# A feed-forward's operand preparation: token halves normed through PSUM, and the first two jobs in another order of products

## The chip, the cores and the metric

One core of one Trainium2 chip runs the whole program as one launch. The metric is the device time in microseconds (us). TensorE is called PE here, VectorE DVE, ScalarE ACT, GpSimd POOL; SP starts the DMAs. [...]

## The reference, cut to what matters

The model has two layers, each a token mixer followed by a feed-forward. There are 512 latent and 256 context tokens of 1024 channels. Only the feed-forward is touched by the change:

```python
def rmsnorm(x, g):
    y = x32 * lax.rsqrt(jnp.mean(x32 * x32, axis=-1, keepdims=True) + NORM_EPS)
    return (y * g.astype(jnp.float32)).astype(x.dtype)
def swiglu(h, w1, w3, w2):
    return (jax.nn.silu(h @ w1) * (h @ w3)) @ w2
...
    x = x + ga_f * swiglu(rmsnorm(x, g_ffn[i]) * (1.0 + sc_f) + sh_f, w1[i], w3[i], w2[i])
```

Layer 0 runs it for all 768 tokens, layer 1 for the 512 latent ones only.

## The kernel before

Activations are stored with the channels on the partitions, in eight tiles of 128 channels, and the tokens along the free axis. An fp32 operand of a matmul is split into a high part (`hi`, a cast by ACT) and a low part (`lo`, the rest, a subtraction on DVE or POOL), and each product is three matmuls in PSUM (L398, L399, L400: hi by hi, hi by lo of the weight, lo by hi). Weights are split likewise (L183 the cast, L188 the lo).

The up-projections `h @ w1` and `h @ w3` are done by a Strassen scheme (Winograd's form). A job is a pair of 128-column blocks of w1 or of w3; the channels are halved (tiles 0 to 3 and 4 to 7) and the tokens are halved, so that the activations are four blocks: B11 and B12 (first half of the channels), B21 and B22 (second half). Seven products p = 1 to 7 replace eight. Products 1 and 2 need B11 and B21, the first token half; p = 3 needs B22; p = 6, 7, 4 and 5 need sums of blocks, called T here: T1 = B12 - B11, T2 = B22 - T1 (p = 6), T3 = B22 - B12 (p = 7), T4 = T2 - B21 (p = 4); p = 5 takes T1. A product is 12 matmuls, 4 chunks of channels by 3, on 384 columns in layer 0 and 256 in layer 1.

PE must be kept busy while the second half's norm and those sums come about. So the four jobs that lead (w1 and w3, two each) do P1 and then P2 together (`first_products`, 48 matmuls each), chunk by chunk, and between the chunks the generator `prepare` is asked for its next steps, as often as the table `PREP` says. The PSUM results of P1 are copied out by ACT (`complete`, L1592), those of P2 wait in PSUM. The first two jobs then do p = 6, 7, 4, 5, 3, and what follows is ordered by a planner with due times (`in_order`), which the change does not touch.

`first_norm` makes the operands of P1 and P2 for the first half: DVE scales a tile (L1471), ACT adds the shift into SBUF (L1479), ACT casts it (L1492), and DVE and POOL take turns at the lo (L1496). `prepare` does the second half: RMS (`rstd`, with L615 its reciprocal), the scaling and shift of both channel halves of one index, T1 (L1515) and T2 (L1517) on DVE, the cast of T2 (L1523), and its lo and T4 on POOL (L1524, L1525). After four indices come T3 (L1528) for all four, and then the operands of p = 7, 4, 5, 3 in four steps (`put`, L1461 the cast, L1462 the lo).

The sums of weight blocks for p = 6 (L225 to L227, a tile S and two others) and p = 7 (L229) are made on DVE by `form`, ahead of their use where room is short; the lo of w1 for p = 7 of the first job is on DVE too. All instructions of an engine run in the order of the code; semaphores tie the engines together. PSUM has 8 banks, dealt out in turn, and a bank's new owner waits for the last reader of the old one. Results go through L1596, L1599, L1603 (sums of products), L1630 and L1634 (sum into a block), L1635 (times the gate).

Of the kernel before, what the change touches and what calls it, by code (L numbers as in the profile page):

```python
# [41 lines left out]
PREP = (0, 1, 1, 2), (1, 1, 1, 2)  # L42
# [4 lines left out]
STEPS = (1, 2, 6, 7, 4, 5, 3)  # L47
NCOL = 0.4219
# [10 lines left out]
class Job:  # L59
# [42 lines left out]
class WeightStream:  # L102
# [6 lines left out]
    def __init__(self, kern, raws, parts):  # L109
# [7 lines left out]

        self.lead, self.dve = {}, {}
# [6 lines left out]

    def add_step(self, job, p, aps):
# [4 lines left out]
        if 1 in self.USES[p] and job.units[1] is None:  # L131
# [19 lines left out]
    def there(self, task):  # L151
# [4 lines left out]
        return all(i in what.raw or what.units[i] in self.raw for i in self.USES[p])  # L156
# [54 lines left out]
    def form(self, job, p):  # L211
# [5 lines left out]
        for i in self.USES[p]:  # L217
            if i not in job.raw:
                job.raw[i] = self.raw.pop(job.units[i])
        n = job.n = job.raw[0].shape[-1] // 2  # L220
        (a11, a12), (a21, a22) = ((t[:, :n], t[:, n : 2 * n]) for t in (job.raw[0], job.raw.get(1, job.raw[0])))
        if p == 6:
# [5 lines left out]
        if p == 7:  # L228
            v.tensor_sub(a12, a12, a11)  # L229
# [1134 lines left out]
class FeedForward:  # L1364
# [10 lines left out]
    def plan(self):  # L1375
# [27 lines left out]
        for j in two:  # L1403
            j.steps = ()
        self.order = [(j, p) for p in (1, 2) for j in lead] + [(j, p) for p in STEPS[2:] for j in two]
# [29 lines left out]
    def begin(self, x, acc, streams, out):  # L1435
# [3 lines left out]
        self.h = [None] * NK  # L1439
# [24 lines left out]
    def scaled(self, rs, st, i):  # L1464

        k = self.k
        if self.h[i] is None:
            self.h[i] = k.act(name="hf")
        t = k.tmp(name="hn")
        for s, sl, at in pieces(st):  # L1470
            k.nc.vector.scalar_tensor_tensor(  # L1471
                t[:, at], self.x[i][:, sl], k.gs[:, self.layer, 1, s, i : i + 1], rs[:, at], op0=OP.mult, op1=OP.mult
            )
        return t

    def shifted(self, t, st, i):
        k = self.k
        for s, sl, at in pieces(st):
            k.nc.scalar.activation(self.h[i][:, sl], t[:, at], AF.Identity, bias=k.mod[:, self.layer, 3, s, i : i + 1])  # L1479

    def first_norm(self):
        st, n = self.streams[0], self.n
        nc = self.k.nc
        rs = yield from self.k.rstd(self.acc[st], st[1])
        yield 0
        for i in range(NK + 1):
            j = i - 1
            if i < NK:
                t = self.scaled(rs, st, i)
            if i > 0:  # L1490
                hi, lo = self.operand(1 + j // 4, j % 4)
                nc.scalar.copy(hi, self.h[j][:, :n])  # L1492
            if i < NK:
                self.shifted(t, st, i)
            if i > 0:
                (nc.gpsimd if j % 2 else nc.vector).tensor_sub(lo, self.h[j][:, :n], hi.bitcast(F32))  # L1496
                yield 0

    def prepare(self):

        st, n = self.streams[1], self.n
        nc = self.k.nc
        v = nc.vector
        rs = yield from self.k.rstd(self.acc[st], st[1], False)
        yield 0

        def block(e, i):
            return self.h[i + 4 * (e // 2)][:, n * (e % 2) : n * (e % 2) + n]

        for i in range(5):  # L1510
            if i < 4:
                ts = [(j, self.scaled(rs, st, j)) for j in (i, i + 4)]
            if i > 0:
                b11, b12, b21, b22 = (block(e, i - 1) for e in range(4))
                v.tensor_sub(b11, b12, b11)  # L1515
                t2 = self.k.tmp(name="T2")[:, :n]
                v.tensor_sub(t2, b22, b11)  # L1517
            if i < 4:
                for j, t in ts:
                    self.shifted(t, st, j)  # L1520
            if i > 0:
# [726 lines left out]
```

## Time and profile before

| | us |
|---|---|
| three runs | 1699.68, 1704.15, 1704.51 |
| median | 1704.15 |
| the profiled execution | 1700.14, of which the span of the trace is 1698.4 |
| PE busy in the span | 1601.1 (94%) |
| DVE, POOL, ACT busy | 1178.8 (69%), 818.6 (48%), 741.9 (44%) |

The span runs from the first instruction to the last; every time below counts from its start. The feed-forward's lead runs from about 448 to 520 us in layer 0 and from 1309 to 1368 us in layer 1. A timeline row is one instruction, or several like it in a row ("x4", with their time together); in brackets stands how long the engine had stood idle before it and which instruction ended that wait. A duration is longer than the distance to the next instruction where work is pipelined: the matmuls of 384 columns last 0.33 us and start every 0.17 us.

### The profile page before, as it was taken

How to read it: one execution, taken by the hardware profiler on the slowest of the kernel's cores; microseconds unless marked ns; L12 is line 12 of the kernel's file. 1: busy time of each engine (PE TensorE's matmuls, PEld its weight loads, DVE VectorE, ACT ScalarE, POOL GpSimd, SP SyncE). 2: the span in 40 equal slices, each digit the busy share in tenths (PEclk: the TensorE clock that was granted, in tenths of full speed). 3: DMA queues.
4: the chain of work that ended last, by engine and by line, in shares of the span. 5: the costliest groups of instructions: out<-in, count | busy, mean ns of one | idle time of the engine just before them, and what ended most of it. 6: DMA issues, size and time to landing. Idle time of an engine off the chain costs nothing. (4 is left out here: it accounts for less than half of the span.)

```text
span 1698.4 us, 26272 instructions
## 1 busy us (share of the span) xinstructions
PE 1601.1 (94%) x9730; PEld 1449.0 (85%) x9730; DVE 1178.8 (69%) x2054; ACT 741.9 (44%) x1437; POOL 818.6 (48%) x601
## 2 busy tenths in 40 slices
PE   6989999999979998999999999999999799999996
PEld 4867788888979987899999997779789789999996
DVE  6866566773777899586766776665666876766685
ACT  5534444653553223242332554444554544344343
POOL 3443232123375556465555623444125676666672
PEclk9999999999989999999999999999999899999998
DMA  9364253353023343434443345422232132332322
GB/s 355 139 199 138 67 160 97 119 170 130 26 76 111 103 134 120 129 125 137 149 137 118 127 161 163 135 73 74 80 131 81 60 115 75 111 114 76 94 87 69
DMA packets 76384, 202.28 MB, mean 119 GB/s; under 512 B 12704, under 2 KB 19488, under 8 KB 75872
## 3 DMA queue, kind: packets, MB, share of 16 engines
q1 hardware_dynamic: 76256, 200.60, 36.5%
q8 instruction: 77, 1.26, 0.3%
q14 instruction: 51, 0.42, 0.1%
HBM read 184.25 MB, written 11.80 MB: 115 GB/s over the span
## 5 line engine op out<-in xcount | busy, mean ns | idle before, releaser
L188 POOL TENSOR_TENSOR wp<-wr,wp 128x512 fp32r<-128x512 f32 (+1 forms) x336 | 465.7, 1399 | 311.0 <-ACT wp L183 306.2
L398 PE MATMUL f<-hp,wp 128*128 128x384 f32 (+1 forms) x1232 | 386.8, 314 | 14.8 <-DVE U L1599 4.2
L399 PE MATMUL f<-hp,wp 128*128 128x384 f32 (+1 forms) x1232 | 387.1, 314 | 10.8 <-DVE wp L188 6.2
L400 PE MATMUL f<-hp,wp 128*128 128x384 f32 (+1 forms) x1232 | 385.2, 313 | 4.0 <-POOL hp L1524 4.0
L183 ACT CAST wp<-wr 128x512 fp32r<-128x512 f32 (+1 forms) x360 | 213.3, 609 | 309.4 <-PE f L400 118.5
L188 POOL TENSOR_TENSOR wl<-wr,wh 128x1024 fp32r<-128x1024 f32 (+2 forms) x75 | 163.8, 2188 | 346.4 <-ACT wh L183 266.4
L398 PEld LDWEIGHTS f<-hp,wp 128*128 128x128 f32 x1232 | 238.0, 193 | 18.8 <-issue 8.2
L399 PEld LDWEIGHTS f<-hp,wp 128*128 128x128 f32 x1232 | 238.4, 193 | 15.3 <-POOL wp L188 8.5
L400 PEld LDWEIGHTS f<-hp,wp 128*128 128x128 f32 x1232 | 238.1, 193 | 5.1 <-POOL hp L1524 5.1
L398 PE MATMUL proj<-h,wh 128*128 128x512 f32 (+1 forms) x456 | 165.0, 362 | 1.0 <-DVE v L404 1.0
L398 PE MATMUL f<-g,wp 128*128 128x512 f32 (+1 forms) x468 | 160.5, 343 | 5.4 <-ACT g L1461 5.4
L400 PE MATMUL f<-g,wp 128*128 128x512 f32 (+1 forms) x468 | 160.5, 343 | 0.0
L399 PE MATMUL f<-g,wp 128*128 128x512 f32 (+1 forms) x468 | 160.3, 342 | 0.0
L399 PE MATMUL proj<-h,wl 128*128 128x512 f32 (+1 forms) x456 | 159.1, 349 | 0.7 <-POOL wl L188 0.7
L400 PE MATMUL proj<-h,wh 128*128 128x512 f32 (+1 forms) x456 | 158.9, 348 | 0.0
L1658 DVE SCALAR_TENSOR_TENSOR x<-f,mod,x 128x512 f32<-128x512 f32 (+1 forms) x130 | 79.0, 622 | 69.5 <-PE f L400 69.3
L398 PEld LDWEIGHTS proj<-h,wh 128*128 128x128 f32 x456 | 86.6, 190 | 25.5 <-issue 6.6
L522 DVE CUSTOM_DVE_ANT_0 adj<-wr,tab 128x1024 bf16<-128x1024 f32 x64 | 104.6, 1653 | 4.1 <-DMA wr<-in_w_adat_dram 4.0
L398 PEld LDWEIGHTS f<-g,wp 128*128 128x128 f32 x468 | 89.1, 190 | 17.0 <-ACT g L1461 6.8
L400 PEld LDWEIGHTS f<-g,wp 128*128 128x128 f32 x468 | 88.9, 190 | 11.2 <-DVE g L1462 1.1
L399 PEld LDWEIGHTS f<-g,wp 128*128 128x128 f32 x468 | 89.1, 190 | 9.9
L399 PEld LDWEIGHTS proj<-h,wl 128*128 128x128 f32 x456 | 86.8, 190 | 11.8 <-POOL wl L188 1.1
(251 smaller groups left out, 3415.2 us busy)
## 6 DMA issues: line engine op xcount, KB each, us to landing
wr<-in_w_dram SPq DMA_DIRECT2D x88, 512.0 KB
wr<-in_w_adat_dram SPq DMA_DIRECT2D x48, 512.0 KB
wr<-in_w_dram SPq DMA_DIRECT2D x80, 256.0 KB
wr<-in_w_ada_dram SPq DMA_DIRECT2D x32, 512.0 KB
ada<-in_w_ada_dram SPq DMA_DIRECT2D x16, 512.0 KB
wr<-in_w_out_dram SPq DMA_DIRECT2D x16, 512.0 KB
tab<-in_rpb_dram SPq DMA_DIRECT2D x12, 512.0 KB
strip<-strips SPq DMA_DIRECT2D x3, 1152.0 KB
```

The lines of the kernel that those rows point to most:

```text
L183: nc.scalar.copy(hi, src)
L188: (nc.vector if vector else nc.gpsimd).tensor_sub(lo, src, hi.bitcast(F32))
L398: mm(out, a[0], b[0], start=start, stop=False)
L399: mm(out, a[1], b[0], start=False, stop=False)
L400: mm(out, a[0], b[1], start=False, stop=stop)
L522: self.nc.vector.tensor_tensor_reduce(out=self.tmp(mybir.dt.bfloat16, D, "adj"), in0=raw, in1=self.tabs[("silu", s)], scale=1.0, scalar=0. ...
L1658: k.nc.vector.scalar_tensor_tensor(xs, ps[:, :n], k.mod[:, self.layer, 5, s, m : m + 1], xs, op0=OP.mult, op1=OP.add)
```

## The change

Four things are done to the preparation of the operands.

- `first_norm` writes the scaled tile into a PSUM bank. ACT reads it twice, once for the fp32 copy and once for the cast, and all the lo are on DVE, from PSUM.
- `prepare` first finishes B22 (a loop over channel tiles 4 to 7: scaled by DVE, scale and shift on ACT, cast on ACT, lo on POOL), which is p = 3's operand. Then come four blocks; in each, ACT writes B12 into a PSUM bank, DVE takes T3 = B22 - bank, turns the bank into T1, ACT copies T1 out, DVE turns the bank into T2, casts and lo follow, and T4 is taken on DVE. Last, the operands of p = 5 and p = 4.
- The first two jobs go p = 3, 7, 6, 4, 5 (`FIRST`). So that p = 3 can come first, all four sums of weight blocks are made ahead of it, and P1's result is copied out twice for these two jobs.
- `PREP` asks for one step fewer after the last chunk of P1.

```diff
-PREP = (0, 1, 1, 2), (1, 1, 1, 2)
+PREP = (0, 1, 1, 1), (1, 1, 1, 2)
+FIRST = (3, 7, 6, 4, 5)
...
-        if p == 6:
+        if p == job.first:
             job.s1 = self.k.tmp(name="S1")[:, :n]
...
-        if p == 7:
+        if p == (3 if job.first == 3 else 7):
             v.tensor_sub(a12, a12, a11)
...
+            if self.held and task[1] is self.held and task[0][1] == self.held.first:
+                self.issue()
+                break
...
-        self.order = [(j, p) for p in (1, 2) for j in lead] + [(j, p) for p in STEPS[2:] for j in two]
+        self.order = [(j, p) for p in (1, 2) for j in lead] + [(j, p) for p in FIRST for j in two]
...
     def first_norm(self):
...
+                ts[i] = k.ps("hn")[:, :n]
...
+                nc.scalar.activation(self.h[j % 4][:, n * (j // 4) : n * (j // 4) + n], t, AF.Identity, bias=shift)
+                nc.scalar.activation(hi, t, AF.Identity, bias=shift)
+                nc.vector.scalar_tensor_tensor(lo, t, shift, hi.bitcast(F32), op0=OP.add, op1=OP.subtract)
...
     def prepare(self):
...
         for i in range(5):
             if i < 4:
+                t = scaled(i + 4)
             if i > 0:
+                hi, lo = self.operand(3, i - 1)
+                nc.scalar.copy(hi, late[i - 1][0])
+                gp.tensor_sub(lo, late[i - 1][0], hi.bitcast(F32))
             if i < 4:
...
+                shifted(late[i][0], t, i + 4)
...
+        bank, ts = None, {0: scaled(0)}
+        for i in range(4):
+            b11, b21, (b22, t3) = self.h[i][:, :n], self.h[i][:, n : 2 * n], late[i]
+            bank = k.ps("T")[:, :n]
+            shifted(bank, ts.pop(i), i)
+            v.tensor_sub(t3, b22, bank)
+            v.tensor_sub(bank, bank, b11)
+            nc.scalar.copy(b11, bank)
+            hi, lo = self.operand(7, i)
+            nc.scalar.copy(hi, t3)
+            gp.tensor_sub(lo, t3, hi.bitcast(F32))
+            if i < 3:
+                ts[i + 1] = scaled(i + 1)
+            v.tensor_sub(bank, b22, bank)
+            hi, lo = self.operand(6, i)
+            nc.scalar.copy(hi, bank)
+            v.tensor_sub(lo, bank, hi.bitcast(F32))
+            v.tensor_sub(b21, b21, bank)
...
         for i in range(4):
+            self.put(self.operand(5, i), self.h[i][:, :n], i % 2)
+            self.put(self.operand(4, i), self.h[i][:, n : 2 * n], 1 - i % 2)
...
         if p == 1:
-            u[2] = self.place(job, 0)
-            self.k.nc.scalar.copy(u[2], ps)
+            for r in (0, 1) if job.first == 3 else (0,):
+                u[2 + r] = self.place(job, r)
+                self.k.nc.scalar.copy(u[2 + r], ps)
...
         elif p == 5:
             add(u[2], u[2], ps)
             self.block(job, 1, 1, ps, u.pop(3))
+            if job.first == 3:
+                self.block(job, 0, 1, ps, u.pop(2), True)
```

The order of PE's and of SP's instructions is the same in both kernels, apart from names. Three places on the other engines, all in layer 0 (layer 1 reads alike):

DVE around the reciprocal of the second half's norm, before. `wr` and `S` are weight blocks, `rs` the norm, `hn` a scaled tile, `hp` an operand of a product; the number behind a name tells tiles apart:

```order
L225 TENSOR_TENSOR S_765_4422<-wr_4268 128x512
L226 TENSOR_TENSOR wr_4268<-wr_3958,wr_4268 128x512
L227 TENSOR_TENSOR wr_3958<-S_765_4422,wr_3958 128x512
L225 TENSOR_TENSOR S_767_4429<-wr_4320 128x512
L226 TENSOR_TENSOR wr_4320<-wr_4027,wr_4320 128x512
L227 TENSOR_TENSOR wr_4027<-S_767_4429,wr_4027 128x512
L615 RECIPROCAL rs_4463<-rs_4463 128x3
L1471 SCALAR_TENSOR_TENSOR hn_4488<-x_3876,gs,rstd_4251 128x384
L1496 TENSOR_TENSOR hp_4490<-hf_4407,hp_4490 128x384
L1471 SCALAR_TENSOR_TENSOR hn_4509<-x_3862,gs,rstd_4462 128x128
```

The same place now (L236, L237, L238, L240 are the old L225, L226, L227, L229; L629 the old L615; L1501 a lo of the first half; L1518 the scaling of the second):

```order
L236 TENSOR_TENSOR S_762_4418<-wr_4268 128x512
L237 TENSOR_TENSOR wr_4268<-wr_3958,wr_4268 128x512
L238 TENSOR_TENSOR wr_3958<-S_762_4418,wr_3958 128x512
L240 TENSOR_TENSOR wr_3958<-wr_3958 128x512
L236 TENSOR_TENSOR S_764_4426<-wr_4318 128x512
L237 TENSOR_TENSOR wr_4318<-wr_4027,wr_4318 128x512
L238 TENSOR_TENSOR wr_4027<-S_764_4426,wr_4027 128x512
L240 TENSOR_TENSOR wr_4027<-wr_4027 128x512
L629 RECIPROCAL rs_4461<-rs_4461 128x3
L1489 SCALAR_TENSOR_TENSOR hn_4485<-x_3876,gs,rstd_4251 128x384
L1501 SCALAR_TENSOR_TENSOR hp_4487<-hn_4404,mod,hp_4487 128x384
L1501 SCALAR_TENSOR_TENSOR hp_4491<-hn_4485,mod,hp_4491 128x384
```

Eight sums of weights stand ahead of the reciprocal instead of six (L229 came later, one between the scalings and one behind the puts), and two lo of the first half behind it instead of one.

ACT around the copies of P1's results (`f` is a PSUM bank, `gate` and `U` where it is copied to), before:

```order
L1479 ACTIVATE hf_4400<-hn_4522,mod 128x128
L1479 ACTIVATE hf_4400<-hn_4522,mod 128x256
L1523 CAST hp_4532<-T_783_4526 128x384
L1592 COPY gate_4536<-f_4433 128x384
L1592 COPY U_4538<-f_4434 128x384
L1592 COPY gate_4540<-f_4435 128x384
L1592 COPY U_4542<-f_4436 128x384
L183 CAST wp_4544<-wr_4027 128x512
L1479 ACTIVATE hf_4308<-hn_4564,mod 128x128
```

And now, with L1523 the scale and shift, L1534 the cast of B22, L1631 the old L1592, L192 the old L183:

```order
L1523 ACTIVATE hf_4533<-hn_4528,mod,gs 128x128
L1523 ACTIVATE hf_4533<-hn_4528,mod,gs 128x256
L1534 CAST hp_4536<-hf_4533 128x384
L1631 COPY gate_4539<-f_4431 128x384
L1631 COPY gate_4541<-f_4431 128x384
L1631 COPY U_4543<-f_4432 128x384
L1631 COPY U_4545<-f_4432 128x384
L1631 COPY gate_4547<-f_4433 128x384
L1631 COPY U_4549<-f_4434 128x384
L192 CAST wp_4551<-wr_4027 128x512
L1523 ACTIVATE T_4572<-hn_4570,mod,gs 128x128
```

Here the whole loop over B22 (12 instructions, of which the last three are shown) stands ahead of the copies; there are six of them instead of four, and the first block's shift comes behind them.

DVE ahead of the lo of w1 for p = 7 (the first `wp` here), before; four T3 and four puts stand between it and the last T2:

```order
L1517 TENSOR_TENSOR T_802_4623<-hf_4487,hf_4350 128x384
L1528 TENSOR_TENSOR hf_4297<-hf_4357,hf_4297 128x384
L1528 TENSOR_TENSOR hf_4301<-hf_4400,hf_4301 128x384
L1528 TENSOR_TENSOR hf_4308<-hf_4407,hf_4308 128x384
L1528 TENSOR_TENSOR hf_4350<-hf_4487,hf_4350 128x384
L1462 TENSOR_TENSOR hp_4645<-hf_4297,hp_4645 128x384
L1462 TENSOR_TENSOR hp_4651<-hf_4308,hp_4651 128x384
L1462 TENSOR_TENSOR hp_4657<-hf_4357,hp_4657 128x384
L1462 TENSOR_TENSOR hp_4663<-hf_4407,hp_4663 128x384
L188 TENSOR_TENSOR wp_4669<-wr_4268,wp_4669 128x512
L229 TENSOR_TENSOR wr_4027<-wr_4027 128x512
```

And now, from the last block on (L1549 is T3, L1550 the bank becoming T1, L1557 the bank becoming T2, L1560 T2's lo, L1561 T4, L1476 a put's lo, L197 the old L188):

```order
L1549 TENSOR_TENSOR hf_4533<-hf_4533,T_4656 128x384
L1550 TENSOR_TENSOR T_4656<-T_4656,hf_4358 128x384
L1557 TENSOR_TENSOR T_4656<-hf_4533,T_4656 128x384
L1560 TENSOR_TENSOR hp_4666<-T_4656,hp_4666 128x384
L1561 TENSOR_TENSOR hf_4358<-hf_4358,T_4656 128x384
L1476 TENSOR_TENSOR hp_4670<-hf_4302,hp_4670 128x384
L1476 TENSOR_TENSOR hp_4679<-hf_4309,hp_4679 128x384
L197 TENSOR_TENSOR wp_4682<-wr_4268,wp_4682 128x512
L197 TENSOR_TENSOR wp_4696<-wr_4268,wp_4696 128x512
```

The lo of w1 still stands behind everything that `prepare` does with T; two puts instead of four stand between.

## Rows read from the trace of the kernel before

**Rows 1.** The page's busy times: us, share of the span, instructions.

```profile
PE 1601.1 (94%) x9730; PEld 1449.0 (85%) x9730; DVE 1178.8 (69%) x2054; ACT 741.9 (44%) x1437; POOL 818.6 (48%) x601
```

**Rows 2.** What PE waited for, whole span: us in total, times, longest us.

```profile
PE f L399 <- DVE wp L188: 6.2, 2, 3.6
```

**Rows 3.** Timeline of PE, layer 0: start, duration, instruction, idle before it.

```profile
462.29 0.44 PE L398 MATMUL f<-hp,wp 128*128 128x384 f32 x1 [1.37 <-ACT gate L1592]
...
482.35 0.69 PE L399 MATMUL f<-hp,wp 128*128 128x384 f32 x1 [3.58 <-DVE wp L188]
482.84 0.53 PE L400 MATMUL f<-hp,wp 128*128 128x384 f32 x1
...
501.62 0.41 PE L398 MATMUL f<-hp,wp 128*128 128x384 f32 x1 [2.15 <-DVE U L1599]
...
516.50 0.44 PE L398 MATMUL f<-hp,wp 128*128 128x384 f32 x1 [0.44 <-DVE g L1462]
```

**Rows 4.** PE alone in stretches of 2 us: busy, granted clock, DMA.

```profile
484.00:486.00 2.00, 2.00 (x8) 0.50 0.00 0
...
488.00:490.00 2.00, 2.00 (x13) 1.00 0.51 197
```

**Rows 5.** Timeline of DVE, layer 0.

```profile
453.42 0.69 DVE L225 TENSOR_TENSOR S<-wr 128x512 f32<-128x512 f32 x1
...
454.93 1.59 DVE L227 TENSOR_TENSOR wr<-S,wr 128x512 f32<-128x512 f32 x1
456.45 0.16 DVE L615 RECIPROCAL rs<-rs 128x3 f32<-128x3 f32 x1
...
460.10 0.55 DVE L1515 TENSOR_TENSOR hf<-hf 128x384 f32<-128x384 f32 x1
...
470.33 5.18 DVE L1528 TENSOR_TENSOR hf<-hf,hf 128x384 f32<-128x384 f32 x4
475.44 5.20 DVE L1462 TENSOR_TENSOR hp<-hf,hp 128x384 fp32r<-128x384 f32 x4
480.56 1.74 DVE L188 TENSOR_TENSOR wp<-wr,wp 128x512 fp32r<-128x512 f32 x1
```

**Rows 6.** Timeline of ACT, layer 0.

```profile
458.21 2.87 ACT L1479 ACTIVATE hf<-hn,mod 128x128 f32<-128x128 f32 x8
...
461.76 0.47 ACT L1592 COPY gate<-f 128x384 f32<-128x384 f32 x1
462.13 0.48 ACT L1592 COPY U<-f 128x384 f32<-128x384 f32 x1
```

**Rows 7.** Timeline, DVE, ACT and DVE in turn, layer 0.

```profile
514.77 0.57 DVE L1635 TENSOR_TENSOR f<-f,gate 128x384 f32<-128x384 f32 x1
...
515.37 0.48 ACT L1461 CAST g<-f 128x384 fp32r<-128x384 f32 x1 [0.71 <-DVE f L1635]
...
515.88 0.56 DVE L1462 TENSOR_TENSOR g<-f,g 128x384 fp32r<-128x384 f32 x1 [0.55 <-ACT g L1461]
```

**Rows 8.** Timeline of DVE, layer 0: two in a row.

```profile
519.29 1.01 DVE L1630 TENSOR_TENSOR gate<-f,gate 128x384 f32<-128x384 f32 x2
```

**Rows 9.** Timeline of PE, layer 1.

```profile
1335.64 0.58 PE L399 MATMUL f<-hp,wp 128*128 128x256 f32 x1 [2.59 <-DVE wp L188]
...
1351.34 0.55 PE L398 MATMUL f<-hp,wp 128*128 128x256 f32 x1 [2.02 <-DVE U L1599]
...
1364.25 0.39 PE L398 MATMUL f<-hp,wp 128*128 128x256 f32 x1 [0.59 <-DVE g L1462]
```

**Rows 10.** PE alone in 2 us of layer 1: busy, granted clock, DMA.

```profile
1352.00:1354.00 2.00, 2.00 (x11) 0.50 0.19 76
```

**Rows 11.** Timeline of DVE, layer 1.

```profile
1316.62 0.15 DVE L615 RECIPROCAL rs<-rs 128x2 f32<-128x2 f32 x1
...
1330.35 3.56 DVE L1462 TENSOR_TENSOR hp<-hf,hp 128x256 fp32r<-128x256 f32 x4
...
1368.69 0.74 DVE L1630 TENSOR_TENSOR gate<-f,gate 128x256 f32<-128x256 f32 x2
```

More of the change, by code (lines that the diff above doesn't have):

```diff
@@ L124, in add, with uses @@
         self.units.append(ap)
+    def uses(self, job, p):
+        return (0, 1) if p == job.first else self.USES[p]
     def add_step(self, job, p, aps):
@@ L155, in there @@
         p = key[1]
-        return all(i in what.raw or what.units[i] in self.raw for i in self.USES[p])
+        return all(i in what.raw or what.units[i] in self.raw for i in self.uses(what, p))
     def need(self, task):
@@ L1510, in prepare, with shifted @@
+        def shifted(out, t, i):
+            for s, _, at in pieces(st):
+                nc.scalar.activation(
+                    out[:, at], t[:, at], AF.Identity,
+                    bias=k.mod[:, self.layer, 3, s, i : i + 1], scale=k.gs[:, self.layer, 1, s, i : i + 1],
+                )
         for i in range(5):
             if i < 4:
-                ts = [(j, self.scaled(rs, st, j)) for j in (i, i + 4)]
+                t = scaled(i + 4)
             if i > 0:
-                b11, b12, b21, b22 = (block(e, i - 1) for e in range(4))
@@ new lines, in prepare @@
+                late[i] = both[:, :n], both[:, n : 2 * n]
+                del both
+                shifted(late[i][0], t, i + 4)
+        del t
+        yield 0
+        bank, ts = None, {0: scaled(0)}
[16 more added lines that the diff above has]
+            v.tensor_sub(b21, b21, bank)
+            late[i] = None
+            del b22, t3, bank
@@ L1547, in product @@
         del w
-        if p == 6 and self.homes and job is self.order[1][0]:
+        if p == FIRST[0] and self.homes and job is self.order[1][0]:
             self.homes.clear()
@@ L1584, in complete @@
     def complete(self, job, p, ps):
-        if p == 6 and job.key in self.waiting:
+        if p in (3, 6) and job.key in self.waiting:
             self.complete(job, 2, self.waiting.pop(job.key))
@@ L1596, in complete @@
             add(u[2], u[2], ps)
+            if 3 in u:
+                add(u[3], u[3], ps)
         elif p == 7:
-            u[3] = self.place(job, 1)
-            add(u[3], u[2], ps)
+            if job.first == 3:
+                add(u[3], u[3], ps)
+            else:
+                u[3] = self.place(job, 1)
+                add(u[3], u[2], ps)
         elif p == 4:
@@ L1604, in complete @@
             self.block(job, 1, 1, ps, u.pop(3))
+            if job.first == 3:
+                self.block(job, 0, 1, ps, u.pop(2), True)
+        elif job.first == 3:
+            add(u[2], u[2], ps)
         else:
@@ L1620, in gate, with block @@
         return self.gates[key]
-    def block(self, job, r, c, ps, u):
+    def block(self, job, r, c, ps, u, done=False):
         k, n = self.k, self.n
@@ L1629, in block @@
         if x == "w1":
[L1630 removed]
+            if not done:
+                nc.vector.tensor_add(gate, ps, u)
             nc.scalar.activation(gate, gate, AF.Silu)
             return
[L1634 to L1635 removed]
+        if not done:
+            nc.vector.tensor_add(ps, ps, u)
+            u = ps
+        nc.vector.tensor_mul(ps, u, gate)
         if c == 1:
```

96 lines of the change are left out of this document (39 added, 57 removed).

## The prediction

> **What bounds the kernel now.** I read the page's busy times first: PE works 94% of the span [rows 1], so a change elsewhere pays or costs only where PE stands. The table of PE's waits, read next, has among its largest the wait of a second matmul for a weight's lo on DVE: 6.2 us in two waits [rows 2]. The timelines show both in the feed-forward's lead, at the start of P7: 3.58 us ending at 482.35 in layer 0, 2.59 ending at 1335.64 in layer 1 [rows 3, 9]. The wait costs more than its length. Behind it the granted clock is 0.50 [rows 4], the next matmul follows after 0.32 us (first pair behind the wait apart) where 0.17 is usual, and that lasts until about 487.6: 16 matmuls, 16 x 0.15 = 2.4 us.
>
> Why is the lo late? DVE is never free from 470.33 to 482.30 [rows 5]: four T3 in 5.18, four puts in 5.20, the lo in 1.74. A subtraction of this size takes 0.55 when it has SBUF to itself (460.10) and a weight block 0.69 (453.42), so POOL beside it more than doubles them. What sets P7's start is thus the length of the preparation's chain, and the question is when that chain ends after the change.
>
> **The change, layer 0, along that chain.** The reciprocal stands at 456.45. Two more weight sums go in ahead of it: 0.69 each alone, 1.59 beside POOL [rows 5]; 1.4 to 3.2. POOL loses its four lo of the first half, so I take 1.2: 457.65.
>
> Behind it come a scaling and two lo of the first half, the second waiting for ACT's two reads of its bank. 0.6 + 1.1 + 0.55 + the first late scaling 0.55 makes 2.8: ACT starts on B22 at 460.45.
>
> ACT's loop over B22: four times two pieces (2.87/4 = 0.72 a pair) and a cast that waits for them (about 0.5) [rows 6], 1.25 a tile, 5.0 in all: 465.45. The P1 copies now stand behind this loop. P2's fourth job needs a bank that they free, so its wait of 1.37 becomes about 5 (466.2 against 462.29) [rows 3]. This is not in the sum: P3 waits later for more.
>
> Six copies at 0.37 (the distance of two rows, [rows 6]) are 2.2, a weight's cast 0.5, the first block's two pieces 0.85: 469.05.
>
> A block is a chain that changes engines: T3 on DVE (0.47 to the next start [rows 8]), the bank to T1 0.55, the copy on ACT 0.47, the bank to T2 0.55, its cast 0.5, then lo and T4 0.47 each, while ACT shifts the next block; a change of engine costs 0.03 [rows 7], waits on the engine's own last result a little more. Together 3.65. Four are 14.6: 483.65. P3's bank was the second block's T, so P3, which needs only the late operand, still starts after block two: 469.05 + 7.3 = 476.3. Its 24 matmuls end at 480.5 at the full clock, 484 at half.
>
> Two puts at 1.3 beside POOL and the lo of w1 at 1.7 [rows 5]: 4.3, so P7's second matmul goes at 487.95 against 482.35: **+5.6 us**, with the same PE work done by then (24 matmuls of P3 instead of P6). The half clock behind the wait stays.
>
> Bounds of this term: the block was never run. If the shift to the next block and T4 hide, it is 3.2; puts and lo alone take 1.6 instead of 4.3; the reciprocal may gain 0.5: +0.6 in all. With blocks of 4.0 and 3.2 for the weights: +9. I take the middle, since the POOL work of the blocks (four lo of T3, two puts, three weights) is queued just there, and the last rows of such a mix are 1.30 and 1.74.
>
> On the other side, PE finds less to wait for behind P7. The wait of 2.15 for U (501.62) goes: the sum it waited for is now needed 24 matmuls after P7 and P6 in place of P7 and P4, with the weight sums that delayed it ahead of time. Three of under 0.5, the last of 0.44 at 516.50 [rows 3], go as PE comes later: -3.5 together. In their place P5 closes two blocks at once: one more product with the gate, cast and lo, 0.57 + 0.48 + 0.56 = 1.6 [rows 7], half of it late for PE: +0.8. Layer 0: 5.6 - 3.5 + 0.8 = **+2.9**.
>
> **Layer 1** goes the same way on 256 columns. DVE operations follow at 0.33 instead of 0.47 [rows 11], a block is 2.7, a put 0.89 (3.56/4), the reciprocal (1316.62) 1.2 later. P7's second matmul goes at 1340.2 against 1335.64: +4.6. The wait of 2.02 at 1351.34 [rows 9] goes, and the half clock after it [rows 10], which cost 15 x 0.095 = 1.4. Small new ones are 0.5, and closing two blocks costs 1.8 where 0.59 was waited: 4.6 - 3.4 + 0.5 + 1.2 = **+2.9**.
>
> What costs nothing: the copies added (counted above), the fp32 second read on ACT and the eight lo on DVE before 450 (DVE and ACT wait there for PE's projections; if that cover were gone the lo would add 4 x 0.55 = 2.2 a layer to the reciprocal). Fewer PREP steps in P1 only move the point at which code of `prepare` is queued.
>
> [...]
>
> **Sum and base.** +5.8 on the profiled execution's 1700.14 is 1705.9. That execution is among the fast ones: the runs' median is 4.0 above it, the mean of all four times 1702.1. Onto the median it is 1710, onto the mean 1708; I say **1709**.
>
> **Rivals.**
>
> Faster: PSUM takes DVE out of POOL's way. At 470 to 482 DVE spends 12.1 us on nine operations that alone take 4 x 0.47 + 4 x 0.47 + 0.69 = 4.5 [rows 5, 8]. Every DVE step of a block has an operand in PSUM, and such steps hold 0.55 to 0.57 [rows 7]. With blocks of 3.2 and puts at 0.47, P7 starts at 483 and PE stands only 2.5 us behind P3. It decides from the point that the clock stays at 1.00 there: 2.4 a layer more. Layer 0: 0.6 - 3.5 + 0.4 - 2.4 = -4.9, layer 1 about -4: 1695; without the clock 1700. Against it: the chain's steps depend on each other, and contention isn't their price. [...]
>
> No change: P7 is late as forecast, but all is given back. Behind P7 the waits that are shown are 3.5 and 5.4 (with the clock); if closing two blocks is hidden, 5.6 - 3.5 = 2.1 and 4.6 - 4.0 = 0.6 stay: 1706.
>
> Slower by more: PE now stands in P2 (5), before P3 (3) and before P7 (4 to 7), so P2 and P3 may run at 0.50 too. P2's remaining 39 matmuls would take 12.5 instead of 6.8 and end at 479, P3 (7.7) at 486.5 and P7's lo would no longer be last: some 1 to 3 a layer on top of the sum, 1714. It decides from the point that P3 ends after 488.
>
> That P3-first doesn't do what it says is part of the forecast: a bank, not its operand, holds it.
>
> **Chances.** Forecast 0.50, faster 0.17, no change 0.23, slower by more 0.07, the page's rule 0.03 (+2.0: 1711). This kernel's runs tell about 0.3%, 5.1 us, from no change; the forecast of +5.8 (by the bounds -3 to +13 over both layers) lies near that line, so I give 0.30 of its 0.50 to slower and 0.20 to the same. Faster 0.17, same 0.43, slower 0.40. The range takes in the no-change case, most of the slower one and a part of the faster one: 1697 to 1717.
>
> **What would show it.** In the new profile: P2's fourth job waiting 4 to 5 us for an ACT copy; blocks 3.65 apart on DVE (the T3 rows); P3's first matmul released by DVE's or ACT's work on block two; P7's second matmul at 488 and 1340, released by the lo of w1, clock 0.50 behind it; no wait of 2 us for a sum of U; a wait of 1 to 2 at P5's end. If P7 starts before 484, or blocks are under 3.3, the forecast is wrong on the fast side; if P3 runs into P7 at half clock, on the slow one.

## The result and the profile after

The changed kernel takes **1713.84 us** (median of four runs, 1713.72 to 1714.49), the kernel before 1704.33 on the same chip (1699.68 to 1704.91): the medians lie 9.5 us apart. The ratio on record is 1.0064, 95% interval [1.0052, 1.0076], which is 8.9 to 13.0 us. The forecast was 1709, in a range of 1697 to 1717: the sign is right, the size is not, +5.8 against +9.5. (The chances were less sure of the sign than the sum: 0.43 for a time that can't be told from no change, 0.40 for slower.)

The page's busy times after, for [rows 1]:

```profile
PE 1605.8 (94%) x9730; PEld 1451.8 (85%) x9730; DVE 1167.3 (68%) x2066; ACT 747.6 (44%) x1449; POOL 800.5 (47%) x585
```

DVE and POOL have less to do than before, by 11.5 and 18.1 us, and the kernel is slower. ACT has 5.7 more. So it isn't the amount of work on the two engines that the change relieves.

The two profiled executions are 13.6 us apart (1700.14 and 1713.72), but 3.0 of that is there before the feed-forward of layer 0 begins: the matmul of the first half's norm starts at 435.13 before and at 438.14 after, in stretches that are alike in both (in the runs below that start moves by -0.1 to 5.5 us). To compare the lead alone, I count from that matmul to the 400th projection matmul recorded behind it; from there on the next 200 take the same time in all kernels of this study (34.85 us in layer 0, 31.7 in layer 1). Timeline of PE, before, the first and the last matmul of the two leads:

```profile
435.13 0.54 PE L619 MATMUL rstd<-cst,rs 128*128 128x128 f32 x3 [0.56 <-DVE rs L615]
...
525.45 0.33 PE L398 MATMUL f<-hp,wp 128*128 128x384 f32 x1
...
1298.69 0.43 PE L619 MATMUL rstd<-cst,rs 128*128 128x128 f32 x2 [0.55 <-DVE rs L615]
...
1371.41 0.28 PE L398 MATMUL f<-hp,wp 128*128 128x256 f32 x1
```

The same view after, with what answers to [rows 3] and [rows 9] between them:

```profile
438.14 0.54 PE L633 MATMUL rstd<-cst,rs 128*128 128x128 f32 x3 [0.56 <-DVE rs L629]
...
470.60 0.69 PE L412 MATMUL f<-hp,wp 128*128 128x384 f32 x1 [5.07 <-ACT gate L1631]
...
481.20 0.41 PE L412 MATMUL f<-hp,wp 128*128 128x384 f32 x1 [0.74 <-DVE hf L1561]
...
489.63 0.44 PE L412 MATMUL f<-hp,wp 128*128 128x384 f32 x1 [4.00 <-ACT wp L192]
...
492.73 0.69 PE L413 MATMUL f<-hp,wp 128*128 128x384 f32 x1 [2.66 <-DVE wp L197]
...
523.72 0.44 PE L412 MATMUL f<-hp,wp 128*128 128x384 f32 x1 [1.17 <-DVE g L1476]
...
532.70 0.34 PE L412 MATMUL f<-hp,wp 128*128 128x384 f32 x1
...
1308.04 0.43 PE L633 MATMUL rstd<-cst,rs 128*128 128x128 f32 x2 [0.55 <-DVE rs L629]
...
1350.56 0.58 PE L413 MATMUL f<-hp,wp 128*128 128x256 f32 x1 [1.92 <-DVE wp L197]
...
1377.16 0.38 PE L412 MATMUL f<-hp,wp 128*128 128x256 f32 x1 [2.25 <-DVE g L1476]
...
1385.05 0.28 PE L412 MATMUL f<-hp,wp 128*128 128x256 f32 x1
```

The lead of layer 0 goes from 90.3 to 94.6 us, that of layer 1 from 72.7 to 77.0: **+4.2 and +4.3, 8.5 of the 9.5**. P7's second matmul (492.73, 1350.56) is 7.4 and 5.6 later than before, counted from the lead's start, and 3.1 and 1.3 of that are given back behind it.

The chain in front of P7. Timeline of DVE after, for [rows 5]: the reciprocal, the first block whole, the first row of the next one, the two puts, the two lo.

```profile
461.05 0.17 DVE L629 RECIPROCAL rs<-rs 128x3 f32<-128x3 f32 x1
...
473.58 0.56 DVE L1549 TENSOR_TENSOR hf<-hf,T 128x384 f32<-128x384 f32 x1 [6.61 <-ACT T L1523]
474.06 0.56 DVE L1550 TENSOR_TENSOR T<-T,hf 128x384 f32<-128x384 f32 x1
474.52 0.54 DVE L1518 TENSOR_TENSOR hn<-x,rstd 128x384 f32<-128x384 f32 x1
475.21 0.56 DVE L1557 TENSOR_TENSOR T<-hf,T 128x384 f32<-128x384 f32 x1
476.32 0.56 DVE L1560 TENSOR_TENSOR hp<-T,hp 128x384 fp32r<-128x384 f32 x1 [0.54 <-ACT hp L1559]
476.80 0.54 DVE L1561 TENSOR_TENSOR hf<-hf,T 128x384 f32<-128x384 f32 x1
477.29 0.56 DVE L1549 TENSOR_TENSOR hf<-hf,T 128x384 f32<-128x384 f32 x1
...
488.38 2.62 DVE L1476 TENSOR_TENSOR hp<-hf,hp 128x384 fp32r<-128x384 f32 x2
490.92 3.43 DVE L197 TENSOR_TENSOR wp<-wr,wp 128x512 fp32r<-128x512 f32 x2
```

And of ACT, for [rows 6]: the late loop's first and last tile, the copies, the weight's cast, the first block.

```profile
463.96 0.99 ACT L1523 ACTIVATE hf<-hn,mod,gs 128x128 f32<-128x128 f32 x2 [1.15 <-DVE hn L1518]
464.98 0.51 ACT L1534 CAST hp<-hf 128x384 fp32r<-128x384 f32 x1
465.40 0.98 ACT L1523 ACTIVATE hf<-hn,mod,gs 128x128 f32<-128x128 f32 x2
...
469.69 0.85 ACT L1631 COPY gate<-f 128x384 f32<-128x384 f32 x2
...
472.43 1.12 ACT L1523 ACTIVATE T<-hn,mod,gs 128x128 f32<-128x128 f32 x2
474.70 0.48 ACT L1551 COPY hf<-T 128x384 f32<-128x384 f32 x1 [1.15 <-DVE T L1550]
```

The reader is to see two things. The DVE operations on a bank last 0.54 to 0.56 each, those at 476.32 and 480.03 with part of their time beside POOL's lo (475.67 to 476.67, 479.38 to 480.39), while the puts, with two operands in SBUF, take 1.31 beside POOL. And DVE waits: 6.61 for ACT's first shift, and in each block 0.54 for a cast. Over the chain, up to some matmuls behind P7's start, the busy times of the engines (stretch, PE, weight loads, DVE, ACT, POOL, clock, DMA), before:

```profile
465.13:484.43 19.30, 12.97 (x56) 11.76 (x55) 19.06 (x20) 9.40 (x21) 17.22 (x14) 0.82 0.08 28
```

and after:

```profile
468.14:494.84 26.70, 16.84 (x71) 15.98 (x72) 18.02 (x28) 17.87 (x40) 13.82 (x12) 0.79 0.05 20
```

DVE worked 99% of that time; now it is idle a third of it, 8.7 us, with less to do. Of these, 5.4 lie ahead of the first T3, where DVE waits for ACT to get through the loop over B22, the copies and the first shift; 3.2 lie in the four blocks, where DVE and ACT hand one bank to and fro.

Of the clock, the engines' busy times in two stretches (the granted clock, a share of full speed, stands third from the end, ahead of DMA):

```profile
492.00:496.00 4.00, 3.27 (x10) 3.27 (x11) 3.37 (x4) 0.47 (x1) 3.49 (x3) 0.50 0.26 92
...
498.00:504.00 6.00, 5.67 (x33) 5.36 (x32) 3.48 (x7) 3.24 (x7) 2.53 (x3) 1.00 0.44 164
```

After the stand of 4.00 and 2.66, P7 starts at a granted clock of 0.50, as it did before [rows 4]. P2 too runs at 0.50 behind its wait of 5.07, from 470 to 476.

### The profile page after: what moved, and what is told of

Its sections match the earlier page's. It is cut to its first block, busy times and chain, and to the rows that moved or that the text cites. A ratio compares the mean times of both kernels' runs of the same rounds, so it can differ in the third digit from the quotient of the medians.

```text
span 1711.9 us, 26308 instructions
## 1 busy us (share of the span) xinstructions
PE 1605.8 (94%) x9730; PEld 1451.8 (85%) x9730; DVE 1167.3 (68%) x2066; ACT 747.6 (44%) x1449; POOL 800.5 (47%) x585
## 5 line engine op out<-in xcount | busy, mean ns | idle before, releaser
L197 POOL TENSOR_TENSOR wp<-wr,wp 128x512 fp32r<-128x512 f32 (+1 forms) x336 | 466.4, 1400 | 323.9 <-ACT wp L192 315.1
L192 ACT CAST wp<-wr 128x512 fp32r<-128x512 f32 (+1 forms) x360 | 212.8, 608 | 321.7 <-PE f L414 119.1
L197 POOL TENSOR_TENSOR wl<-wr,wh 128x1024 fp32r<-128x1024 f32 (+2 forms) x75 | 163.6, 2186 | 349.5 <-ACT wh L192 284.9
L1709 DVE SCALAR_TENSOR_TENSOR x<-f,mod,x 128x512 f32<-128x512 f32 (+1 forms) x130 | 79.1, 624 | 72.9 <-PE f L414 72.7
```

Of the source, the lines that this page charges most:

```text
L192: nc.scalar.copy(hi, src)
L197: (nc.vector if vector else nc.gpsimd).tensor_sub(lo, src, hi.bitcast(F32))
L1709: k.nc.vector.scalar_tensor_tensor(xs, ps[:, :n], k.mod[:, self.layer, 5, s, m : m + 1], xs, op0=OP.mult, op1=OP.add)
```

## The experiments

Each line: the time, the kernel before beside it, the ratio with its interval, and the two leads of the profiled run.

| run | edit | us | before | ratio | lead 0, lead 1 |
|---|---|---|---|---|---|
| before | | 1704.33 | | | 90.3, 72.7 |
| after | the change | 1713.84 | 1704.33 | 1.0064 [1.0052, 1.0076] | 94.6, 77.0 |
| e1 | + P7's weights early | 1715.75 | 1704.19 | 1.0069 [1.0055, 1.0083] | 98.7, 76.6 |
| e2 | + copies ahead of the late loop | 1711.45 | 1704.19 | 1.0044 [1.0027, 1.0061] | 93.9, 77.1 |
| e3 | + first norm in SBUF | 1709.21 | 1704.19 | 1.0034 [1.0020, 1.0047] | 93.2, 76.6 |
| e4 | + P6 first | 1708.00 | 1704.19 | 1.0021 [1.0011, 1.0031] | 91.6, 74.5 |
| e5 | + both, so blocks alone | 1705.01 | 1703.88 | 1.0008 [0.9997, 1.0020] | 91.0, 73.9 |
| e6 | before + first norm in PSUM | 1705.01 | 1703.88 | 1.0020 [1.0010, 1.0029] | 91.7, 73.5 |
| e7 | after, P3, P6, P7 | 1708.11 | 1703.88 | 1.0034 [1.0021, 1.0047] | 93.3, 74.6 |
| e8 | before + P7's weights early | 1706.62 | 1703.88 | 1.0023 [1.0012, 1.0034] | 91.5, 73.0 |
| e9 | e8, sums held back | 1702.63 | 1703.26 | 0.9996 [0.9986, 1.0005] | 91.7, 71.3 |
| e10 | e1, sums held back | 1713.15 | 1703.26 | 1.0062 [1.0047, 1.0077] | 96.6, 76.1 |
| e11 | e5 + e9's edits | 1712.34 | 1703.26 | 1.0059 [1.0046, 1.0071] | 99.6, 73.2 |
| e12 | e5, blocks overlapped | 1707.34 | 1702.03 | 1.0034 [1.0021, 1.0046] | 92.3, 74.3 |

The sum of the two leads against before (8.5 for the change, 3.1 for e4, 0.0 for e9, 9.7 for e11) follows the ratio times 1704 (10.9, 3.6, -0.7, 10.1) to within 2.5 us in every line. So what the edits do to the time, they do for the most part in the leads.

**e1, the weights early.** Rooms outside the weights' own for P7's two weights let their cast and lo go ahead of the blocks. `elsewhere` takes them from the tiles in which the operands stand:

```diff
                 for j in jobs[:2]:
                     j.home[FIRST[0]] = j.home[1]
+                    j.home[7] = k.w.elsewhere
```

> The changed kernel, with room of their own for P7's two weights, so that their casts and lo are done ahead of the first block instead of behind the last. Theory (the lo of w1 at the end of DVE's chain sets P7's start, and the half clock behind it is part of the price): no wait for a weight's lo before P7, which starts within 2 us of block four's end; the block chain itself moves 1.0 us later by two casts. Behind P7 the chain of g takes over, so 2 to 4 us a layer come back: 1706 to 1709 us, against 1713.8 for the changed kernel. Rival (PE waits for the operands of the blocks, the weight only happens to come last): the time stays within 2 us of 1713.8.

No gain. P7 no longer waits for its weight, but two other waits appear. Timeline of PE in e1, then of DVE just ahead of the second:

```profile
485.00 0.66 PE L412 MATMUL f<-hp,wp 128*128 128x384 f32 x1 [4.86 <-DVE hf L1561]
...
503.16 0.66 PE L412 MATMUL f<-hp,wp 128*128 128x384 f32 x1 [8.03 <-DVE gate L1680]
```

```profile
497.45 1.75 DVE L236 TENSOR_TENSOR S<-wr 128x512 f32<-128x512 f32 x1
...
500.91 1.63 DVE L238 TENSOR_TENSOR wr<-S,wr 128x512 f32<-128x512 f32 x1
502.46 0.54 DVE L1680 TENSOR_TENSOR gate<-f,gate 128x384 f32<-128x384 f32 x1
```

P3 waits 4.86 and starts 2.6 later than in the changed kernel, counted from the lead's start, since the weights' work now delays the blocks; and P6 waits 8.03 for the sum of P2's result, which frees its bank and stands behind three weight sums that now find room ahead of it.

**e2, the copies first.** P1's copies go ahead of ACT's loop over B22, one line:

```diff
-PREP = (0, 1, 1, 1), (1, 1, 1, 2)
+PREP = (0, 1, 1, 0), (2, 1, 1, 2)
```

> The changed kernel, with the loop over B22 asked for after P2's first chunk instead of after P1, so that the copies of P1 stand ahead of it on ACT. Theory (P2's wait of 5 us is hidden behind the block chain): that wait falls to 1 us or less and P2 runs at the full clock, yet P7 moves by no more than the 1 us that ACT stood idle ahead of the loop: 1711 to 1714 us. Rival (PE's standing in P2, and the half clock behind it, is the price): 3 to 5 us a layer come back, 1704 to 1708.

P2's wait of 5.07 goes, and P3 waits 6.71 instead of 0.74. The leads change by -0.7 and +0.1: the wait of 5 was hidden, as the forecast had it. (The interval of its ratio overlaps that of the change.)

**e3, the first half's norm through SBUF.** `first_norm` as before, the rest as changed:

```diff
-                ts[i] = k.ps("hn")[:, :n]
+                t = k.tmp(name="hn")[:, :n]
...
-                nc.scalar.activation(hi, t, AF.Identity, bias=shift)
-                nc.vector.scalar_tensor_tensor(lo, t, shift, hi.bitcast(F32), op0=OP.add, op1=OP.subtract)
+                nc.scalar.copy(hi, h)
+                (nc.gpsimd if j % 2 else nc.vector).tensor_sub(lo, h, hi.bitcast(F32))
```

> The changed kernel, with the first half's norm as in the kernel before (scaled in SBUF, POOL and DVE taking turns at the lo). Theory (the first half's part delays the last update of x by 1.1 us and with it the reciprocal and the whole chain): the reciprocal comes 0.5 to 1 us earlier a layer, 1711.5 to 1713. Rival (the price is in the first half's norm): about 1705.

4.6 us faster than the change (1709.21 against 1713.84), of which the leads show 1.8 (-1.4 and -0.4): between theory and rival. The theory's reason fails too: the matmul of the second half's norm comes 0.3 earlier in layer 0 and 0.3 later in layer 1. P2's wait falls from 5.07 to 2.35.

**e4, P6 first.** Everything else as changed; the P3-first branches fall away with it (the copies made twice, the extra weight sum ahead of the reciprocal, the two blocks closed by P5):

```diff
-FIRST = (3, 7, 6, 4, 5)
+FIRST = (6, 7, 4, 5, 3)
```

> The changed kernel, with the first two jobs in the old order 6, 7, 4, 5, 3, all else kept (so one copy of P1 less for each of them and six weight sums ahead of the reciprocal). Theory (P7's start is set by DVE's chain whichever product goes ahead of it, and 24 matmuls fit in either way): P7's second matmul within 1.5 us of where it is in the changed kernel, 1711 to 1715 us. Rival (P3 ahead fills time that would else be idle): 3 us or more slower, 1717 and above.

1708.0: 6 us faster than the change, better than theory and rival had it. This is the largest single part, and it was not in my account as a cost. The matmul of the second half's norm comes 21.7 us after the lead's start (462.27 - 440.62) where the changed kernel needs 23.2 (461.37 - 438.14), in layer 1 17.8 against 19.4: 1.6 less in each layer, for the two weight sums (one a job) that need not stand ahead of the reciprocal. P7's second matmul comes 2.3 earlier in layer 0 (52.3 after the lead's start against 54.6), and no longer waits for its weight. And P6 takes the blocks as they come. Timeline of PE in e4:

```profile
481.35 0.41 PE L412 MATMUL f<-hp,wp 128*128 128x384 f32 x1 [0.95 <-DVE hf L1561]
483.92 0.44 PE L412 MATMUL f<-hp,wp 128*128 128x384 f32 x1 [1.28 <-ACT hp L1559]
487.62 0.69 PE L412 MATMUL f<-hp,wp 128*128 128x384 f32 x1 [2.67 <-ACT hp L1559]
```

**e5, both reversions,** so that of the change the blocks in PSUM stay (the edits are those of e3 and e4):

> The changed kernel with both reversions at once: P6 first (FIRST = 6, 7, 4, 5, 3, no second job state) and the first half's norm through SBUF as in the kernel before. What is left of the change is the blocks in PSUM, job by job order and the half tiles. Theory, costs add: 1713.8 - 6 (P6 first alone) - 4.6 (SBUF norm alone) = 1703 to 1704, the kernel before's time; the blocks in PSUM then cost nothing. Rival, both reversions take away the same wait, since either makes PE reach P7 with less standing: 1706 to 1708. Second rival, the blocks in PSUM are themselves worth something once freed: 1699 to 1702.

1705.01, a ratio that can't be told from 1, halfway between the first theory and its rival; the leads are +0.7 and +1.2. By the leads the blocks cost 1.8 us; by the times that can't be told from nothing. They do not pay, though DVE has less to do. **e6, the first norm through PSUM in the kernel before** (the reverse of e3's diff):

> The kernel before with only the first half's norm through PSUM (scaling into a bank, two ACT reads, every lo on DVE). Theory: it costs by itself what undoing it gave, 4.6 us in all, as DVE's reciprocal for the second half and ACT's reads come later at the head of the preparation's chain: 1707 to 1709, with P7's second matmul in layer 0 some 2 later. Rival: in the kernel before the reciprocal is held by the sums ahead of it and not by these lo, so it costs nothing: 1703 to 1705.

A ratio of 1.0020 [1.0010, 1.0029], 1.7 to 4.9 us (the medians are only 1.1 apart), of which the leads show +1.4 and +0.8. It costs by itself; by the leads less than the theory's 4.6, which the interval doesn't exclude. P7's second matmul comes 1.3 later in layer 0.

**e7, P3, then P6, then P7:**

```diff
-FIRST = (3, 7, 6, 4, 5)
+FIRST = (3, 6, 7, 4, 5)
...
+        if job.first == 3 and p == 7:
+            return (1,)
         return (0, 1) if p == job.first else self.USES[p]
```

> The changed kernel with FIRST = (3, 6, 7, 4, 5): P3 first as changed, but P6, which takes the blocks one by one, before P7, which takes all four and the late weight. Theory: the cost of P3 first is the stretch in which PE stands before P7 with nothing to pace it, and the half clock that falls on useful work behind it; P6 in between is paced by the blocks and covers weight and puts: 1706 to 1709, at or below 1708.0 of P6 first. Rival: P3 first costs by what comes with it, the second copies, a third sum ahead of the reciprocal and two blocks closed by one product: then the order behind it is worth under 1 us, 1712 to 1714. P6 at half clock in the whole stretch would end it between, 1710.

1708.11, in the theory's range, but not by its mechanism: P6 isn't paced by the blocks, it stands for its own weight, as P7 did. Timeline of PE in e7:

```profile
489.02 0.44 PE L414 MATMUL f<-hp,wp 128*128 128x384 f32 x1 [4.03 <-ACT wp L194]
...
491.57 0.69 PE L415 MATMUL f<-hp,wp 128*128 128x384 f32 x1 [2.10 <-POOL wp L199]
```

The leads gain 1.3 and 2.4 on the change by this order. P6's lo comes from POOL, but DVE still makes P7's two (3.44 us from 490.31) and gets to its first sum no earlier: 56.2 us after the lead's start, against 56.1 in the changed kernel. So it isn't an earlier DVE that makes the gain; 0.5 of it in each layer is there at the second matmul behind P3, and where the rest comes from was not separated.

**e8, the weights early in the kernel before** (e1's line there):

> The kernel before with rooms of their own for P7's weights of the first two jobs, so that their cast and lo can be formed ahead of the preparation's chain. Theory: P7's second matmul is then released by the puts or blocks, some 1.7 us (the lo of w1) earlier in layer 0 and 1.3 in layer 1, with less half clock behind it: 1700 to 1703. Rival, the wait moves as it did in the changed kernel with the same edit (P3 4.86, then P6 8.03 behind three sums formed ahead): 1704 to 1707.

1706.62: the rival, at its upper end. P7's wait of 3.58 goes, and P4's first product (the 145th matmul of the lead's products; the expectation of e9 calls it P6's second) waits 6.04 for the gate sum behind three weight sums. **e9 and e10** hold those sums back until P7 of w1 is done, in the kernel before and in the changed one:

```diff
-                if AHEAD and isinstance(task[1], Job) and self.there(task):
+                if AHEAD and not self.calm and isinstance(task[1], Job) and self.there(task):
```

> The kernel before with P7's weights in rooms of their own, and the weight sums of the later jobs not formed ahead until w1's P7 is done. Theory: with the weights early the wait moved to P6's second product (6.04 in layer 0, 4.96 in layer 1), because P2's sum, which frees the PSUM bank, stood behind three weight sums of 1.7 formed ahead; with those held back it comes 5.0 and about 3.5 earlier: lead of layer 0 some 4 and of layer 1 some 3 shorter than with early weights alone, 1698 to 1701, below the kernel before. Rival, DVE's queue as a whole sets the lead, so the sums only move to the next wait (the sum of U or the gate): 1703 to 1706.

> The changed kernel with the same two edits. Theory: P6's wait of 8.03 (layer 0) and 7.03 (layer 1) behind three sums formed ahead shrinks by about 5 and 3.5; with P3 first the rest is the blocks' chain: 1715.8 - 8 = 1706 to 1709, still above the kernel before with the same edits by 5 or more. Rival, DVE's queue as a whole sets the lead: 1711 to 1714. If P3 first costs nothing once the weights are early, it comes within 2 us of the kernel before with the same edits.

e9: 1702.63, ratio 0.9996 [0.9986, 1.0005]. The wait of 6.04 shrinks to 1.02 as the theory says; then, timeline of PE in e9,

```profile
498.04 0.69 PE L399 MATMUL f<-hp,wp 128*128 128x384 f32 x1 [4.25 <-DVE g L1463]
```

PE waits 4.25 for a lo of g on DVE. The time lies between theory and rival; layer 0 shows the rival (its lead is no shorter than e8's), layer 1 half the theory's gain (1.7). e10 at 1713.15 is the rival's: its waits, 8.03 before, are now 3.07 and 3.16, and P3's is 4.66 still. The change as a whole costs as much here as without early weights: 10.5 us between e9 and e10.

**e11, e5 with the same two edits:**

> P6 first and the first half's norm through SBUF, so that of the change only the blocks in PSUM stay (1705.0 so far), with the same two edits. Theory: its P7 waits only 0.87 for the weight's lo and its gate sum then stands behind nothing, so the edits give 1 to 2 here: 1702 to 1704. Rival: without the weights in the chain's tail, the two weights of 1.8 and a sum of 1.8 that stand between the puts and the gate sum go, and P7 and P6 come 3 earlier in each layer: 1698 to 1700.

1712.34, 7 us slower than e5, outside all that was expected. Timeline of DVE in e11 ahead of the first block, then of ACT:

```profile
468.66 1.36 DVE L198 TENSOR_TENSOR wp<-wr,wp 128x512 fp32r<-128x512 f32 x1 [6.59 <-ACT wp L193]
469.94 1.77 DVE L241 TENSOR_TENSOR wr<-wr 128x512 f32<-128x512 f32 x1
471.63 0.54 DVE L1519 TENSOR_TENSOR hn<-x,rstd 128x384 f32<-128x384 f32 x1
```

```profile
472.27 1.07 ACT L1524 ACTIVATE T<-hn,mod,gs 128x128 f32<-128x128 f32 x2 [3.12 <-DVE hn L1519]
```

The lo and the sum of the early weights stand in DVE's queue ahead of the scaling of the first block, and DVE gets to them only when ACT has cast the weight. ACT's first shift waits 3.12 for that, and P7's second matmul is 4.0 later than in e5, of the 8.6 by which layer 0's lead is longer. The rest comes behind it, and it starts with a room and not with the queue. Timeline of ACT in the kernel before, the last casts of the puts, then one of them in e11:

```profile
475.60 2.17 ACT L1461 CAST hp<-hf 128x384 fp32r<-128x384 f32 x5 [0.77 <-DVE hf L1528]
```

```profile
494.52 0.51 ACT L1476 CAST hp<-hf 128x384 fp32r<-128x384 f32 x1 [4.27 <-PE f L414]
```

The cast writes an operand's tile, and all that PE does with such a tile is to read it: the cast waits 4.27 for a room that PE must first be done with, and DVE then stands 5.42 for the cast. In e8 and e9 such a cast waits 3.06 and 2.82 for PE, in e1 and e10 about 0.4, in the kernels without early weights not at all, and nowhere in layer 1. The early weights took those rooms. None of the expectations counted with that.

**e12, e5 with the blocks overlapped.** The next block's shift goes ahead of this one's second cast, this one's lo behind the next one's differences:

```diff
+            if left:
+                v.tensor_sub(left[0], left[1], left[2])
...
             if i < 3:
-                ts[i + 1] = scaled(i + 1)
+                banks.append(k.ps("T")[:, :n])
+                shifted(banks[0], ts.pop(i + 1), i + 1)
             v.tensor_sub(bank, b22, bank)
             hi, lo = self.operand(6, i)
             nc.scalar.copy(hi, bank)
-            v.tensor_sub(lo, bank, hi.bitcast(F32))
             v.tensor_sub(b21, b21, bank)
...
+            left = lo, bank, hi.bitcast(F32)
```

> P6 first and the first half's norm through SBUF (1705.0 so far), with the blocks in PSUM overlapped by hand: the next block's shift goes to ACT ahead of this block's second cast, its scaling to DVE ahead of time, and this block's lo behind the next block's two differences, in a second bank. Same instructions, another order. Theory, the blocks are a chain of latencies between DVE and ACT, DVE working 17.1 of 22.3 us there and ACT 14.4: six DVE steps of 0.47 a block would allow 2.85, so the distance of two blocks falls from 3.71 to 3.0 or less, P7's second matmul comes 2 to 3 earlier in layer 0 and 1.5 in layer 1; by a third to a half of it given back behind P7: 1701 to 1703, at or below the kernel before. Rival, ACT's queue is the bound, so the distance stays over 3.5: 1704 to 1706. Second rival, the distance falls but the waits move to the gate sum and the g casts behind P7, as with the weights: 1704 to 1706 with a distance under 3.2.

1707.34 against 1702.03: slower than all three expected; the distance stays over 3.5 as the first rival says, but not by its reason. Timeline of DVE in e12, T4 of the first block and the T3 of the second and third:

```profile
470.37 0.55 DVE L1566 TENSOR_TENSOR hf<-hf,T 128x384 f32<-128x384 f32 x1 [1.22 <-ACT hp L1565]
...
471.31 0.55 DVE L1551 TENSOR_TENSOR hf<-hf,T 128x384 f32<-128x384 f32 x1
...
475.74 0.55 DVE L1551 TENSOR_TENSOR hf<-hf,T 128x384 f32<-128x384 f32 x1
```

The blocks are 4.36, 4.43 and 3.88 apart instead of 3.71. T4 only reads the bank, and so does ACT's cast, yet T4 waits 1.22 for it, and the cast now stands behind the next block's shift. By these rows the distance of two blocks is set by the turns that the engines take at a bank, and this order made the turns longer; whether an order with a distance of 3.0 exists was not shown. No version here beats the kernel before by more than can be measured.

## Why the forecast had the sign and missed the size

What held. The price does lie in the chain in front of P7, and the signs named for it are all there: P2's fourth job waits 5.07 for an ACT copy (about 5), blocks are 3.71 apart (3.65) and 2.7 in layer 1, P3 is released by block two, two puts take 2.62 (2.6), a lo of a weight 1.7 (1.7), P7 starts behind that lo at half clock (0.50), the 2-us waits for U are gone, and the waits for what P5 closes are 1.17 and 2.25 (1 to 2). e2 shows P2's wait hidden, as said. The rival "faster" fell by its own rows: the steps on a bank do hold 0.56 beside POOL, but they depend on ACT, and DVE's saved time turns into DVE's idle time. The +2.0 (1711) to which the chances give 0.03 is shown by no run: DVE's steps on a bank last 0.54 to 0.56 after, and a subtraction from SBUF 0.55 before (460.10) [rows 5]. The measured 1713.84 is the number of the rival "slower by more", 1714, but not by its reason: P2 does run 18 matmuls at half clock (0.50), yet P3 waits only 0.74 behind it instead of 3, runs at the full clock (1.00) and ends at 485.6, not after 488.

What failed, first: the size of P7's term, +5.6 in layer 0 against 7.4 measured. Counted from the lead's start with before's 435.13 (3.0 less than the rows after show), the error builds up so:

- the reciprocal: 457.65 said, 458.04 measured: +0.4;
- the late loop: 1.25 a tile said, 1.43 measured (463.96 to 469.69 for four, 5.73 instead of 5.0): +0.7, and its start +0.1. I took a pair of pieces at 0.72, from a row of eight that add the shift alone and run one behind the other [rows 6]. The pair now takes 1.02. Its pieces scale as well (`gs` among their inputs) and last 0.09 to 0.10 longer each; and the cast, which needs their result, starts 0.03 after their end, where ACT otherwise starts an instruction 0.09 ahead of the end of the one before;
- the first block's shift in two pieces, 0.85 said, 1.15 from 472.43 to the first T3: +0.3, for the scale again, and since the second piece starts only 0.03 after the end of the first;
- four blocks: +0.2.

That is 1.7 of 1.8. ACT's pieces by shape, before (the row of eight) and after (the late loop): how many, busy us, mean ns.

```profile
L1479 ACT ACTIVATE hf<-hn,mod 128x256 f32<-128x256 f32 x4 | 2.0, 494 | 0.0
L1479 ACT ACTIVATE hf<-hn,mod 128x128 f32<-128x128 f32 x4 | 1.6, 390 | 0.0
```

```profile
L1523 ACT ACTIVATE hf<-hn,mod,gs 128x256 f32<-128x256 f32 x4 | 2.3, 586 | 0.0
L1523 ACT ACTIVATE hf<-hn,mod,gs 128x128 f32<-128x128 f32 x4 | 2.0, 492 | 1.1 <-DVE hn L1518 1.1
```

So the largest part is one fault: an ACT operation was costed from rows of another one. The scale adds 0.19 a pair, by an estimate from these rows 0.95 over the five pairs ahead of the first T3. The rest of the loop's and the blocks' error is that durations of operations that run one behind the other were used for operations that wait for each other. Layer 1 is off by less, 5.6 against 4.6.

Second, what is given back behind P7: 2.7 was the forecast for layer 0 and 1.7 for layer 1; 3.1 and 1.3 were measured. In layer 1 the wait of 2.25 stands where 0.59 was waited before, 1.7 more and not the 1.2 charged; the 1.73 was there already (1.79 before, ending at 1362.00). The rival "no change" names 5.4 of waits there and reckons with 4.0; the rows it shows give 4.0 (2.02, 0.59 and 1.4 for the clock), the trace has 6.0 of waits alone (0.89, 2.02, 1.79, 0.59, 0.72).

Third, P3 first was costed by its copies, its weight sums and its closings, but never compared with the same blocks behind P6 first. From the leads of the experiments, undone one after the other, the change's 8.5 us are: the order P3, P7, P6 in place of P3, P6, P7 3.7 (after to e7); P3 first with what comes with it 1.7 (e7 to e4); the first norm through PSUM 1.2 (e4 to e5); the blocks 1.8 (e5 to before). By the medians, each beside its own runs of the kernel before, they are 5.3, 0.4, 2.7 and 1.1. They differ with the order in which the parts are undone. With the norm undone first (after to e3 to e5), the leads give 1.8 to the norm and 4.9 to P3 first, and the medians 4.5 and 3.9. So by the leads P3 first, with the order behind it, is the largest part and more than half either way; by the medians that depends on the way, and the intervals, some 2 us to either side, don't settle it. P3 first needs a fourth weight sum of each of two jobs ahead of the reciprocal, 1.6 us on the chain; and P3's 24 matmuls, which need no block, are over before the chain is, so that PE stands and then runs P7 at half clock (0.50), where P6 spreads its work over the blocks.

My theory after the result, that the late weight of P7 is the last wait and so the price, fell with e1, e8 and e11: taken from the chain's tail, the weight's work goes to its head, or frees room for other sums that stand in the way. Layer 0 of e1 and e8 to e11 fits another account, that DVE's and ACT's queues from the reciprocal to the first gate sums are one chain, so that a wait that is taken away comes back at the next matmul that needs DVE. It is not shown. In e8, e9 and e11 the shortage of rooms took part, and no run gives the early weights room without taking it from the operands. And in layer 1, where no such cast waits for PE, the leads with early weights and the sums held back are shorter (one profiled run each): by 1.4 in e9 against before, 0.9 in e10 against the change, 0.7 in e11 against e5. Not settled either is what lies outside the leads, 1 to 2.5 us in several lines; the median of the changed kernel is 1.0 further from before than its leads, by the ratio 2.4.

## What to carry to other kernels

A lighter engine isn't a shorter chain: when work that one engine did without a gap is turned into steps that two engines do in turn, cost it by the distance of dependent steps (here 1.43 for three ACT instructions that I took at 1.25, from rows at full flow and without the scale; take the price from rows with the same operands), and count what stands in the queue ahead of the first step as part of it. When products are reordered so that one can start early, ask what PE does between the end of that product and the end of the chain: a product that takes the blocks one by one bridges the chain, one that needs none of them doesn't. Before moving a late operand, look at which queue it moves to the head of, and whose room it takes.

## What was not expected of the hardware

Two engines that only read the same PSUM bank took turns: DVE's difference waited 1.22 us for ACT's cast of the same bank in e12, and the semaphores were set so by the program, so whether the bank itself would have forced it is open. An ACT activation that takes a scale from a tile beside its shift lasts longer than one with the shift alone: 492 ns against 390 on 128 columns, 586 against 494 on 256. An ACT instruction that needs the result of the one before starts 0.03 us after its end (464.98 after), one that doesn't 0.09 ahead of it (465.40). So two pieces with scale and a cast of their result came every 1.43 us, where eight pieces without scale took 2.87 [rows 6], 0.72 for two.
